# The triangular inverse of each chunk in blocks of 16 joined by products, in a two-layer streaming encoder step

## The chip, the core and the metric

The kernel runs on one core of a Trainium2 chip, as one launch in float32. The metric is device time in microseconds (us); lower is better. TensorE (in the profile PE, its weight loads PEld) multiplies matrices into PSUM; VectorE (DVE), ScalarE (ACT) and GpSimd (POOL) do the elementwise work; SyncE (SP) issues the DMAs. Each engine takes its instructions strictly in the order of the program, and waits on semaphores for those of the others.

## The reference

One step of a streaming encoder with two layers over 1024 prompt tokens and 64 sample tokens, width 1024. Layer 0 is an RWKV-7 time mixing with 16 heads of 64 features and a SwiGLU FFN; layer 1 is windowed attention and another FFN. What matters here is the recurrence of layer 0 (S is a 64 x 64 state for each head):

```python
def step(s, inp):
    r_t, w_t, k_t, v_t, a_t, b_t = inp
    sa = jnp.einsum('bhvk,bhk->bhv', s, a_t)
    s = s * w_t[:, :, None, :] + sa[..., None] * b_t[:, :, None, :] + v_t[..., None] * k_t[:, :, None, :]
    return s, jnp.einsum('bhvk,bhk->bhv', s, r_t)
...
    s_fin, y = lax.scan(step, s0.astype(f32), seq_in)
```

## The kernel before

The 1088 tokens are cut into 17 chunks of 64: eight of the first half of the prompt (A), eight of its second half and one of the sample stream (B). In a chunk the recurrence is solved at once: with T the strict triangle of the products of the b and a vectors, U = W U0, where W = D (I - T D)^-1 and D holds 1 / |kk|^2. So each chunk needs 16 inverses of 64 x 64 triangles, one a head. The heads are held as eight pairs, the even one on partitions 0 to 63 and the odd one on 64 to 127.

For each chunk, `prep` loads the operands, forms the decays and the four triangles of each head (tile `G`, in the code X) by products into PSUM and a mask; `prep2` calls `inverse`, which makes W, and turns the keys (`BT`); `chain` takes the state M through the chunk in four sets of products (U0, Y, U = W U0, the new state); `post` normalises the output Y and turns it back. `recur` runs these so that `prep` and `prep2` of a chunk are emitted beside `chain` and `post` of the chunk ahead.

`inverse` first copies the two diagonal 32 x 32 blocks of each triangle, each four times (`st`, ScalarE, L191), and turns them in blocks of 32 x 32 on VectorE (L196), so that a lane (partition) holds one block and one fourth of its rows: 2 blocks x 16 heads x 4 is 128 lanes. Then it substitutes backwards, two columns at a time, with a multiplication (L216) and a sum (L220) for each of two halves of the rows: 28 of each a chunk. The result is turned back (`WD` and its transpose `XD`) and copied to the diagonal blocks of W. The block beside them comes from two sets of sixteen 32 x 32 products on TensorE: one with the off-diagonal block of T (`N12`, tile `in12`) into `QT`, one with WD into W.

The rest of the kernel is dense work: projections of the time mixing for A, then, beside the recurrence of A, those for B; then, beside the recurrence of B, the output projection and the FFN of A; then attention and the FFNs. Each dense product is three float32r products (lines L422 to L424, PSUM tile `dp`), with the weights split into two parts by ScalarE (L382) and by VectorE or GpSimd (L383).

The order of the instructions on each engine is not written out. A scheduler places them when the program is built, by a priority number and its own estimate of when operands are ready. `recur` gives its products the priority of the stage (1 for A, 3 for B) and most of its other work a lower one (2.5 and 4.5). So a change in one function moves the dense work around it too. A matmul in float32 (not float32r) is recorded twice in the trace.

Lines that the prediction names: L191 (copies into `st`), L196, L198, L205, L206, L208 (turn, scaling, first step and start values), L216 and L220 (substitution), L237 (turn to XD), L247 and L248 (copies of QT), L254 and L255 (last copies into W), L73 and L77 (the helpers through which all products and transposes of the recurrence pass, told apart by tiles: `p_rc` from `r_ixd` are the joins), L110 (norms), L311 (end of the GpSimd part of `post`).

Of the kernel before, what the change touches and what calls it, by code (L numbers as in the profile page):

```python
# [9 lines left out]
F32 = mybir.dt.float32  # L10
# [38 lines left out]
class Rwkv:  # L49
    """The chunked WKV-7 recurrence: chunks of 64 tokens, 16 heads in 8 pairs."""  # L50
# [31 lines left out]
    def start(self):  # L82
        """the part of W that stays zero"""
        nc = self.nc
        self.W = self.sb.tile([128, 8, 64], F32, name="W", tag="W", bufs=1)
        nc.gpsimd.memset(self.W, 0.0)

    def prep(self, ch):
        """all that does not need the state; heads 2j on partitions 0-63, heads 2j + 1 on 64-127"""
# [13 lines left out]
        # 1 / |kk|^2 as the lanes of inverse() hold it: [(parity, half of the tokens, 4 times, pair), token]  # L103
# [30 lines left out]
        # kk a / P and -kk Pex without the norm of kk, whose square inverse() divides by  # L134
# [3 lines left out]
        # r k r_k  # L138
# [3 lines left out]
        # the four triangles of each head: [(b, k) of the key, (a, r) of the query]  # L142
# [10 lines left out]
        # sum(r k r_k) v  # L153
# [7 lines left out]
    def prep2(self, d):  # L161
# [4 lines left out]
        # the strict triangle of b is spent: a takes its place  # L166
# [13 lines left out]
    def inverse(self, X, nl):  # L180
        """D (I - T D)^-1 of the strict triangles T, transposed, with D = 1 / |kk|^2: first the blocks of 32 by
        substitution, a lane for each block and each fourth of its rows, then the block beside them"""
# [4 lines left out]
        st = self.t([128, 1024], "f4", 2)  # L187
        for q in range(4):
            d = 32 * (q % 2)
            src = Xh[d:d + 32, :, q // 2, d:d + 32].rearrange("p j t -> p t j").unsqueeze(2).broadcast_to([32, 32, 4, 8])  # L190
            S.copy(st[32 * q:32 * q + 32].rearrange("p (t g j) -> p t g j", g=4, j=8), src)  # L191
# [370 lines left out]
def tile_stream_step(ctx: ExitStack, tc: tile.TileContext, I, O):  # L562
# [8 lines left out]
    c = {}  # L571
# [841 lines left out]
```

## Time and profile before

| | us |
|---|---|
| three runs | 3085.4, 3092.2, 3096.0 |
| median | 3092.2 |
| span of the profiled execution | 3098.9 |
| TensorE busy | 2948.1 |
| VectorE busy | 1905.6 |
| ScalarE busy | 1371.1 |
| GpSimd busy | 921.6 |

The profiled execution is one run by itself; of its time the profile has only the span, from the first to the last instruction. The profile's groups give for each line and shape the union of the busy time, the mean duration of one and the idle time of the engine ahead of them. Matmuls overlap, so the mean of one is longer than the step from one to the next. The granted clock is the share of TensorE's full clock that its throttle let through.

### The profile page before, as it was taken

Reading aid. Unit: us, or ns where it says so; the run is one execution under the profiler, and the core shown is the slowest. Engines: PE = TensorE matmul, PEld = TensorE weight load, DVE = VectorE, ACT = ScalarE, POOL = GpSimd, SP = SyncE. Lnnn points to the kernel's source line nnn. Section 1 sums busy time; section 2 is a strip of 40 time slices with the busy share of each in tenths; the row PEclk is TensorE's granted clock in tenths of the full one; section 3 lists DMA queues with packets and bytes.
Section 4 is the critical chain, followed back from the end, with each engine's and each line's share of the span. In section 5 each row is a group of like instructions: output and inputs, shape, how many; then the busy total and the mean of one; then the engine's idle time right before and its main releaser. Section 6 shows DMA issues by size and latency. Waiting matters only on the chain. (4 is left out here: it accounts for less than half of the span.)

```text
span 3098.9 us, 52449 instructions
## 1 busy us (share of the span) xinstructions
PE 2948.1 (95%) x20126; PEld 2520.6 (81%) x20126; DVE 1905.6 (61%) x3964; ACT 1371.1 (44%) x2489; POOL 921.6 (30%) x768
## 2 busy tenths in 40 slices
PE   6899898998899999999999999999999999999998
PEld 5677677886677777887778999888667889899998
DVE  8887788968898984356654333565555334633334
ACT  6767655434555442344553222344454233322222
POOL 6464233423333322224311222243111222322221
PEclk9998778988899999999999999999999999999999
DMA  4645443334223224332212222222122332322222
GB/s 143 171 121 152 116 123 91 106 99 143 79 83 96 86 66 127 103 112 84 70 45 69 82 82 82 76 84 82 55 65 65 96 96 75 102 83 83 85 85 69
DMA packets 262051, 289.16 MB, mean 93 GB/s; under 512 B 125028, under 2 KB 143972, under 8 KB 261800
## 3 DMA queue, kind: packets, MB, share of 16 engines
q1 hardware_dynamic: 261800, 285.81, 30.8%
q8 instruction: 158, 2.59, 0.3%
q14 instruction: 93, 0.76, 0.1%
HBM read 243.18 MB, written 41.16 MB: 92 GB/s over the span
## 5 line engine op out<-in xcount | busy, mean ns | idle before, releaser
L422 PE MATMUL dp<-xh,wh 128*128 128x288 f32 (+2 forms) x3480 | 1184.5, 342 | 26.5 <-DVE hx L951 7.0
L423 PE MATMUL dp<-xl,wh 128*128 128x288 f32 (+2 forms) x3480 | 1174.9, 338 | 9.5 <-DVE xl L415 6.9
L424 PE MATMUL dp<-xh,wl 128*128 128x288 f32 (+2 forms) x3480 | 1172.3, 337 | 0.0
L382 ACT CAST wh<-wr 128x512 fp32r<-128x512 f32 x730 | 445.8, 619 | 821.7 <-PE dp L423 635.2
L422 PEld LDWEIGHTS dp<-xh,wh 128*128 128x128 f32 x3480 | 669.2, 193 | 100.5 <-DVE hx L951 9.9
L423 PEld LDWEIGHTS dp<-xl,wh 128*128 128x128 f32 x3480 | 669.9, 193 | 72.3 <-DVE xl L415 8.8
L424 PEld LDWEIGHTS dp<-xh,wl 128*128 128x128 f32 x3480 | 670.2, 193 | 61.4 <-issue 5.6
L383 DVE TENSOR_TENSOR wl<-wr,wh 128x512 fp32r<-128x512 f32 x487 | 377.6, 779 | 444.2 <-ACT wh L382 435.5
L383 POOL TENSOR_TENSOR wl<-wr,wh 128x512 fp32r<-128x512 f32 x243 | 336.0, 1383 | 997.3 <-ACT wh L382 894.1
L422 PE MATMUL dp<-mh,wh 128*128 128x288 f32 (+1 forms) x808 | 255.0, 316 | 3.6 <-DVE hx L951 2.6
L424 PE MATMUL dp<-mh,wl 128*128 128x288 f32 (+1 forms) x808 | 254.6, 315 | 0.0
L423 PE MATMUL dp<-ml,wh 128*128 128x288 f32 (+1 forms) x808 | 253.8, 314 | 0.0
L951 DVE TENSOR_TENSOR a_xB<-dp,a_xB 128x288 f32<-128x288 f32 x352 | 158.1, 456 | 82.4 <-PE dp L424 81.9
L932 DVE TENSOR_TENSOR st<-st,dp 128x288 f32<-128x288 f32 (+1 forms) x132 | 70.0, 531 | 216.8 <-PE dp L424 216.4
L934 POOL TENSOR_TENSOR xl<-st,xh 128x288 fp32r<-128x288 f32 (+1 forms) x102 | 101.2, 993 | 334.2 <-ACT xh L933 322.1
L422 PEld LDWEIGHTS dp<-mh,wh 128*128 128x128 f32 x808 | 152.5, 189 | 13.5 <-DVE hx L951 3.8
L424 PEld LDWEIGHTS dp<-mh,wl 128*128 128x128 f32 x808 | 152.4, 189 | 8.1 <-issue 1.8
L423 PEld LDWEIGHTS dp<-ml,wh 128*128 128x128 f32 x808 | 152.6, 189 | 6.8 <-issue 0.8
L951 DVE TENSOR_TENSOR hx<-dp,hx 128x512 f32<-128x512 f32 x176 | 119.8, 685 | 48.2 <-PE dp L424 47.9
L191 ACT COPY r_f<-r_G 32x1024 f32<-32x1024 f32 x68 | 134.7, 1981 | 32.5 <-DVE r_G L152 21.2
L216 DVE TENSOR_TENSOR r_f<-r_f,r_f 128x60 f32<-128x60 f32 (+5 forms) x476 | 117.5, 278 | 0.5
L930 ACT ACTIVATE st<-dp 128x288 f32<-128x288 f32 (+1 forms) x132 | 62.2, 471 | 93.2 <-PE dp L424 92.8
(344 smaller groups left out, 4003.3 us busy)
## 6 DMA issues: line engine op xcount, KB each, us to landing
wr<-in_ffn_in SPq DMA_DIRECT2D x352, 256.0 KB
wr<-in_ffn_out SPq DMA_DIRECT2D x176, 256.0 KB
wr<-in_rkv SPq DMA_DIRECT2D x90, 256.0 KB
wr<-in_rwo SPq DMA_DIRECT2D x32, 256.0 KB
wr<-in_wq SPq DMA_DIRECT2D x32, 256.0 KB
wr<-in_wo SPq DMA_DIRECT2D x32, 256.0 KB
r_r_s<-s_s SPq DMA_DIRECT2D x17, 256.0 KB
r_sv<-s_vt SPq DMA_DIRECT2D x17, 256.0 KB
```

Of the source, the lines that this page charges most:

```text
L191: S.copy(st[32 * q:32 * q + 32].rearrange("p (t g j) -> p t g j", g=4, j=8), src)
L216: V.tensor_tensor(out=Z[:, h, 1:3, r0:4, 0:j], in0=Z[:, h, a, r0:4, j:j + 2].rearrange("p r c -> p c r").unsqueeze(3).broadcast_to([128, 2 ...
L382: nc.scalar.copy(h, x)
L383: (nc.gpsimd if self.turn % 3 == 0 else nc.vector).tensor_tensor(out=l, in0=x, in1=h, op=ALU.subtract)
L422: self.nc.tensor.matmul(ps, lhsT=wh, rhs=xh, start=i == 0, stop=False)
L423: self.nc.tensor.matmul(ps, lhsT=wh, rhs=xl, start=False, stop=False)
L424: self.nc.tensor.matmul(ps, lhsT=wl, rhs=xh, start=False, stop=i == last)
L930: S.activation(t[o], p, AF.Silu)
L932: V.tensor_tensor(out=t[o], in0=t[o], in1=p, op=ALU.mult)
L934: G.tensor_tensor(out=a.lo[:, q], in0=t[o], in1=a.hi[:, q], op=ALU.subtract)
L951: V.tensor_tensor(out=self.x[m][:, q], in0=p, in1=self.x[m][:, q], op=ALU.add)
```

## The change

The diagonal blocks that are substituted are now 16 x 16: 4 blocks x 16 heads x 2 lanes a block. The copies into `st` and the turn have 512 elements in place of 1024; the lanes of the two blocks of a 32 x 32 square are told apart by masks (`self.e`, made once in `start`). The substitution has seven steps, each one multiplication and one sum over all rows, no longer in two halves. The 16-blocks are joined to 32 by two new sets of 32 products with 16 columns (tile `r_ixd` with X or `in12` into `Q1`, then `Q1` with WD), with a copy by ScalarE between and a sum and a turn by VectorE behind. The joint of 32 to 64 is as before, but takes its operand from X where the heads are even. The constant `xl0` is built on the chip. Comments and docstrings are left out as well. The core of the diff (`...` marks what is left out):

```diff
     def start(self):
         nc = self.nc
-        self.W = self.sb.tile([128, 8, 64], F32, name="W", tag="W", bufs=1)
-        nc.gpsimd.memset(self.W, 0.0)
+        one = lambda shape, n: self.sb.tile(shape, F32, name=n, tag=n, bufs=1)
+        self.W = one([128, 8, 64], "W")
+        self.Q1 = one([128, 8, 32], "Q1")
+        G.memset(self.Q1, 0.0)
+        self.e = one([128, 8], "lanes")
...
-        nl = self.t([128, 32], "nl", 3)
-        V.transpose(out=nl, in_=n4)
+        n2, nl = self.t([128, 32], "n2"), self.t([128, 16], "nl", 3)
+        V.transpose(out=n2, in_=n4)
+        V.tensor_scalar(out=nl, in0=n2[:, 0:16], scalar1=self.e[:, 0:1], scalar2=None, op0=ALU.mult)
+        V.scalar_tensor_tensor(out=nl, in0=n2[:, 16:32], scalar=self.e[:, 1:2], in1=nl, op0=ALU.mult, op1=ALU.add)
...
     def inverse(self, X, nl):
-        st = self.t([128, 1024], "f4", 2)
+        st = self.t([128, 512], "f4", 2)
...
-        N12 = self.t([128, 8, 32], "in12")
-        S.copy(N12[0:32], Xh[0:32, :, 0, 32:64])
-        S.copy(N12[64:96], Xh[0:32, :, 1, 32:64])
+        N1 = self.t([128, 8, 64], "in12")
+        S.copy(N1[64:128], X[0:64, 8:16, 0:64])
...
-        for j in range(30, 0, -2):
+        for j in range(14, 0, -2):
             a, b = (0, 3) if j % 4 else (3, 0)
-            part = [(h, (j // 4 + 1 - h) // 2) for h in range(2) if (j // 4 + 1 - h) // 2 < 4]
-            for h, r0 in part:
-                n = 4 - r0
-                V.tensor_tensor(out=Z[:, h, 1:3, r0:4, 0:j],
...
-            for h, r0 in part:
-                V.tensor_reduce(out=Z[:, h, b, r0:4, 0:j], in_=Z[:, h, min(a, 1):min(a, 1) + 3, r0:4, 0:j].rearrange("p c r j -> p r j c"),
-                                axis=AX.X, op=ALU.add)
+            r0, n = j // 2, 8 - j // 2
+            V.tensor_tensor(out=Z[:, 1:3, r0:8, 0:j],
+                            in0=Z[:, a, r0:8, j:j + 2].rearrange("p r c -> p c r").unsqueeze(3).broadcast_to([128, 2, n, j]),
+                            in1=N0[:, j:j + 2, 0:j].unsqueeze(2).broadcast_to([128, 2, n, j]), op=ALU.mult)
+            V.tensor_reduce(out=Z[:, b, r0:8, 0:j], in_=Z[:, min(a, 1):min(a, 1) + 3, r0:8, 0:j].rearrange("p c r j -> p r j c"),
+                            axis=AX.X, op=ALU.add)
...
+        for e in range(2):
+            V.tensor_scalar(out=XX.rearrange("p (r s) -> p r s", r=8)[:, :, 16 * e:16 * e + 16], in0=XL, scalar1=self.e[:, e:e + 1], scalar2=None, op0=ALU.mult)
...
+        turn()
...
+        ps = self.pc()[:, 0:128].rearrange("p (a b) -> p a b", a=8)
+        for j in range(8):
+            for q in range(4):
+                o = slice(32 * q, 32 * q + 32)
+                self.mm(ps[o, j, :], lhsT=T(q, j, slice(o.start % 64, o.start % 64 + 32)), rhs=XD[o, j, 0:16], start=True, stop=True)
+        S.copy(Q1[:, :, 0:16], ps)
+        ps = self.pc()[:, 0:128].rearrange("p (a b) -> p a b", a=8)
+        for j in range(8):
+            for q in range(4):
+                o = slice(32 * q, 32 * q + 32)
+                self.mm(ps[o, j, :], lhsT=Q1[o, j, :], rhs=WD[o, j, 16:32], start=True, stop=True)
+        V.tensor_tensor(out=WD[:, :, 16:32], in0=ps, in1=WD[:, :, 16:32], op=ALU.add)
+        turn()
+        V.tensor_scalar(out=W[:, :, 0:32], in0=WD, scalar1=self.e[:, 2:3], scalar2=None, op0=ALU.mult)
+        S.activation(W[:, :, 32:64], WD, AF.Copy, scale=self.e[:, 3:4])
...
-    for n in ("tri", "mask", "bd", "xl0"):
+    for n in ("tri", "mask", "bd"):
```

What this does to the order is seen at three places. First VectorE, in the substitution of a chunk of the second half, before (`r_f` are the tiles NL and Z of the code; the last number is the shape of what is written):

```order
L216 TENSOR_TENSOR r_f_518_9089<-r_f_518_9089,r_f_517_9086 128x2x3x8
L216 TENSOR_TENSOR r_f_518_9089<-r_f_518_9089,r_f_517_9086 128x2x3x4
L220 TENSOR_REDUCE r_f_518_9089<-r_f_518_9089 128x3x8
L220 TENSOR_REDUCE r_f_518_9089<-r_f_518_9089 128x3x4
L216 TENSOR_TENSOR r_f_518_9089<-r_f_518_9089,r_f_517_9086 128x8x6
L216 TENSOR_TENSOR r_f_518_9089<-r_f_518_9089,r_f_517_9086 128x8x2
L220 TENSOR_REDUCE r_f_518_9089<-r_f_518_9089 128x4x6
L220 TENSOR_REDUCE r_f_518_9089<-r_f_518_9089 128x4x2
```

and in such a chunk of the changed kernel (L420 splits a weight of the FFN, L318 copies U):

```order
L237 TENSOR_REDUCE r_f_612_9831<-r_f_612_9831 128x2x12
L234 TENSOR_TENSOR r_f_612_9831<-r_f_612_9831,r_f_611_9827 128x2x3x10
L237 TENSOR_REDUCE r_f_612_9831<-r_f_612_9831 128x3x10
L234 TENSOR_TENSOR r_f_612_9831<-r_f_612_9831,r_f_611_9827 128x2x4x8
L237 TENSOR_REDUCE r_f_612_9831<-r_f_612_9831 128x4x8
L234 TENSOR_TENSOR r_f_612_9831<-r_f_612_9831,r_f_611_9827 128x2x5x6
L420 TENSOR_TENSOR wl_12257<-wr_12258,wh_12256 128x512
L237 TENSOR_REDUCE r_f_612_9831<-r_f_612_9831 128x5x6
L234 TENSOR_TENSOR r_f_612_9831<-r_f_612_9831,r_f_611_9827 128x2x6x4
L237 TENSOR_REDUCE r_f_612_9831<-r_f_612_9831 128x6x4
L318 COPY r_sv_9691<-p_rc_9731 64x8x64
```

Two steps of each kind before each result was used have become one. Over the whole program VectorE has 3326 instructions in place of 3964.

Then TensorE at the joins, before, in the second half (`p_rc` from `r_ixd` is a join; `p_ry` belongs to `chain`):

```order
L422 MATMUL dp_11805<-xh_11200,wh_11799 128x512
L73 MATMUL p_ry_8953<-r_M_8689,r_AR_8555 64x64 x16
L73 MATMUL p_rc_8830<-r_ixd_8801 32x32
L423 MATMUL dp_11805<-xl_11201,wh_11799 128x512
L424 MATMUL dp_11805<-xh_11200,wl_11800 128x512
L422 MATMUL dp_11805<-xh_11206,wh_11799 128x512
L73 MATMUL p_rc_8954<-r_sv_8949,r_G_8567 64x64 x16
L73 MATMUL p_rc_8830<-r_ixd_8801 32x32 x15
```

and in the changed kernel, from the end of the first new set of products past the second (`Q` is Q1, `p_rp` from `r_AR` makes the triangles of the next chunk):

```order
L73 MATMUL p_rc_9478<-r_ixd_9474,r_in_565_9444 32x16 x2
L73 MATMUL p_rp_9623<-c_bd,r_rt_9620 64x2 x8
L73 MATMUL p_rp_9662<-r_AR_9649,r_BK_9650 128x128 x4
L459 MATMUL dp_12097<-xh_11691,wh_12091 128x512
L460 MATMUL dp_12097<-xl_11692,wh_12091 128x512
L461 MATMUL dp_12097<-xh_11691,wl_12092 128x512
L73 MATMUL p_rc_9512<-r_ixd_9474,Q_2522 32x16 x32
L73 MATMUL p_rp_9663<-r_AR_9649,r_BK_9650 128x128 x4
L73 MATMUL p_rp_9674<-r_AR_9649,r_BK_9650 128x128 x4
```

Between the two new sets stand eight small products, four of the triangles and three dense ones; TensorE has 18350 instructions in place of 17262.

Third, the dense products between chunks, counted in TensorE's order from the last product of U of one chunk to that of another:

| | before | changed |
|---|---|---|
| first to eighth chunk (A) | 986 | 603 |
| eighth to ninth | 236 | 629 |
| ninth to seventeenth (B) | 913 | 572 |

The dense work is the same; less of it stands beside the recurrence and more behind it.

More of the change, by code (lines that the diff above doesn't have):

```diff
@@ new lines, in inverse @@
+        one = N0[:, 32:512:66]
+        N0 = N0.rearrange("p (t s) -> p t s", t=16)
+        NL = N0[:, :, 0:16]
+        V.scalar_tensor_tensor(out=NL, in0=NL, scalar=self.e[:, 0:1], in1=N0[:, :, 16:32], op0=ALU.mult, op1=ALU.add)
+        V.tensor_tensor(out=NL, in0=NL, in1=mid(nl, 16), op=ALU.mult)
+        ev = N0.rearrange("p (a two) b -> p a two b", two=2)[:, :, :, 0:16]
+        Z = self.t([128, 4, 8, 16], "f4", 2)
+        tm = Z[:, 0]
+        V.tensor_tensor(out=tm, in0=bc(one, 16), in1=ev[:, :, 0, :], op=ALU.mult)
@@ new lines, in inverse @@
+            V.tensor_reduce(out=Z[:, b, r0:8, 0:j], in_=Z[:, min(a, 1):min(a, 1) + 3, r0:8, 0:j].rearrange("p c r j -> p r j c"),
+                            axis=AX.X, op=ALU.add)
+        XL = Z[:, 0]
+        q4 = lambda x: x.rearrange("p r (q f) -> p r q f", f=4)[:, :, :, 0:2]
+        V.tensor_copy(q4(XL), q4(Z[:, 3]))
+        xe = XL.rearrange("p r (a two) -> p r a two", two=2)
+        tm = Z[:, 1, :, 0:8]
+        V.tensor_tensor(out=tm, in0=xe[:, :, :, 1], in1=mid(one, 8), op=ALU.mult)
```

69 lines of the change are left out of this document (31 added, 38 removed).

## The prediction

> **What bounds the kernel now.** I read the page first: its span, the busy shares, and its forty slices.
>
> ```profile
> span 3098.9 us, 52449 instructions
> ...
> PE 2948.1 (95%) x20126; PEld 2520.6 (81%) x20126; DVE 1905.6 (61%) x3964; ACT 1371.1 (44%) x2489; POOL 921.6 (30%) x768
> ...
> DVE  8887788968898984356654333565555334633334
> ...
> PEclk9998778988899999999999999999999999999999
> ```
>
> TensorE is busy 95% of the span. VectorE is nearly full only in the first 16 slices, and only there does the granted clock fall: that is where the recurrence runs. The profiled execution has a span of 3098.9 us, 6.7 above the median of the three times (3092.2); no other time of it is given. I sum the change in us and add it to the median.
>
> VectorE's timeline shows when the last piece of each chunk's inverse W is written (L255; start, length), 17 times:
>
> ```profile
> 343.84 0.42 DVE L255 COPY W<-p_rc 32x256 f32<-32x256 f32 x1 [0.24 <-ACT W L254]
> ...
> 1173.52 0.42 DVE L255 COPY W<-p_rc 32x256 f32<-32x256 f32 x1 [0.29 <-ACT W L254]
> ```
>
> The eighth ends at 672, the ninth, which opens the second half, at 788. So I cut the span at these four times and asked for the busy time of each stretch (columns: stretch, length, then busy us of PE, PEld, DVE, ACT, POOL, then granted clock).
>
> ```profile
> 265.00:344.00 79.00, 63.80 (x517) 54.87 (x516) 55.71 (x145) 55.98 (x84) 21.68 (x21) 0.81 0.48 145
> 344.00:672.00 328.00, 308.36 (x3115) 266.50 (x3115) 271.26 (x750) 179.41 (x289) 109.05 (x77) 0.84 0.39 106
> 672.00:788.00 116.00, 93.48 (x640) 73.64 (x638) 85.41 (x173) 51.65 (x73) 38.24 (x29) 0.82 0.44 126
> 788.00:1174.00 386.00, 373.46 (x3276) 287.64 (x3276) 347.76 (x922) 192.86 (x266) 133.26 (x100) 0.93 0.27 84
> ...
> 1217.00:1317.00 100.00, 100.00 (x433) 81.20 (x431) 37.44 (x54) 28.66 (x48) 23.73 (x19) 1.00 0.44 128
> 2700.00:2800.00 100.00, 100.00 (x753) 100.00 (x752) 38.36 (x76) 26.16 (x50) 20.72 (x19) 1.00 0.26 83
> ```
>
> Two stretches are start-ups (265 to 344 and 672 to 788), in which one chunk is prepared with none to run beside it. Two are steady: seven chunk periods of the first half (A), eight of the second (B). The last two rows are dense work alone: 0.231 us for a matmul of 512 columns, 0.133 for one of 288. With these rates I take the dense work out of a steady stretch. Two groups of TensorE of the first steady stretch, then one of the second:
>
> ```profile
> L422 PE MATMUL dp<-xh,wh 128*128 128x290 f32 x284 | 95.0, 337 | 4.6 <-ACT st L792 4.6
> ...
> L752 PE MATMUL dp<-xh,wl 64*128 64x290 f32 x16 | 8.2, 515 | 0.0
> ...
> L422 PE MATMUL dp<-xh,wh 128*128 128x512 f32 x294 | 126.5, 432 | 6.5 <-DVE st L932 4.0 <-DVE hx L951 2.5
> ```
>
> A holds three groups like the first (852) and six like the second (96): 948 at 0.133 are 126 us, so 328 - 126 = 202 us, 28.9 a chunk, go to the recurrence. B holds three like the third (880): 203 us, which leaves 183, or 22.9 a chunk. The recurrent work of a chunk is the same in both. TensorE stands idle 328 - 308.4 = 19.6 us in A (2.8 a chunk) and 12.5 in B (1.6); the rest of the difference goes with the clock, 0.84 against 0.93. So TensorE bounds both, and VectorE, at 83% and 90%, sets some of A's waits.
>
> **The change, part by part.** What goes is VectorE's and ScalarE's (groups of the whole span):
>
> ```profile
> L216 DVE TENSOR_TENSOR r_f<-r_f,r_f 128x60 f32<-128x60 f32 (+5 forms) x476 | 117.5, 278 | 0.5
> ...
> L220 DVE TENSOR_REDUCE r_f<-r_f 128x30 f32<-128x90 f32 (+5 forms) x476 | 97.9, 237 | 0.8
> ...
> L208 DVE TENSOR_TENSOR r_f<-c_xl,r_nl 128x256 f32<-128x256 f32 x34 | 26.1, 808 | 0.3
> ...
> L198 DVE TENSOR_TENSOR r_f<-r_f,r_nl 128x1024 f32<-128x1024 f32 x17 | 25.0, 1470 | 0.2
> ...
> L196 DVE STREAM_TRANSPOSE r_f<-r_f 128x1024 f32<-128x1024 f32 x17 | 21.1, 1243 | 34.8 <-ACT r_f L191 34.8
> ...
> L237 DVE STREAM_TRANSPOSE r_ixd<-r_ixd 128x256 f32<-128x256 f32 x17 | 7.5, 440 | 0.4
> ...
> L191 ACT COPY r_f<-r_G 32x1024 f32<-32x1024 f32 x68 | 134.7, 1981 | 32.5 <-DVE r_G L152 21.2
> ```
>
> The substitution goes from 28 multiplications and 28 sums a chunk to 7 and 7: three quarters of 215 us, or 161. The rows of 1024 and 256 elements shrink to half or a quarter: of their 72 us some 35 go. The new masks, a third turn (440 ns by L237) and the add from PSUM give about 25 back. VectorE is thus relieved of about 170 us, 10 a chunk. The substitution is now one dependent sequence, no longer two halves in turn; in the order other work of VectorE stands between some of its steps, and where none does a step waits for the one ahead, in room that VectorE then has. ScalarE's four copies halve: 67 us, 4 a chunk. None of this is time by itself where TensorE is full. SyncE loses one constant's load; the once-only preparation of the lanes (a dozen small VectorE instructions) stands beside dense work at 265 us; I cost both at nothing. Without that cover the preparation would be some 3 us.
>
> What comes is TensorE's: 96 small products a chunk in place of 32, so 1088 more. The nearest row is the present block of sixteen 32x32 products (x32 because each is recorded twice):
>
> ```profile
> 1141.78 1.22 PE L73 MATMUL p_ry<-r_M,r_AR 64*64 64x64 f32 x22
> 1142.93 0.69 PE L73 MATMUL p_rc<-r_ixd,r_in 32*32 32x32 f32 x32
> 1143.56 0.33 PE L77 MATMUL p_rp<-c_id,r_BK 64*128 64x64 f32 x2
> ...
> 586.85 1.06 PE L73 MATMUL p_rc<-r_ixd,r_in 32*32 32x32 f32 x32
> ```
>
> From its start to the next start it takes 0.63 us at the full clock and 0.99 at half. For 64 more that is 2.5 us a chunk, or 4.0 at half clock. The new ones have half the columns and lie on four row groups in place of two: at best half the price, 1.25. They can't cost less than nothing, since each is issued in order. I take 2.0, nearer the row: **+34 us** for 17 chunks (21 to 56, most chunks being at the full clock).
>
> By the Trainium skill, TensorEngine Tiling (Array Packing), Tiling Modes, Key Properties, a change of the tiling mode drains the engine. In the rows above the block begins 0.07 us before the one ahead of it ends, and so does the one behind it, so the trace shows no such drain at these two edges. By the rule two more blocks would bring four more drains a chunk; at 0.19 us each, the length of one product, that would be 13 us more.
>
> The new joins also add two waits to each inverse: TensorE for ScalarE's copy of Q1, and for VectorE's sum and turn. In the order of the changed program, products of the next chunk's G and a few dense ones stand between, so I cost them at nothing; without that cover each is about one copy of 0.4 us, 14 us in all.
>
> What goes of TensorE's waits, from its waits in three stretches (us in all, times, longest):
>
> ```profile
> PE p_ry L77 <- POOL r_yc L311: 5.5, 1, 5.5
> PE p_rc L73 <- ACT r_ixd L247: 4.7, 1, 4.7
> PE p_rc L73 <- DVE r_ixd L237: 3.0, 1, 3.0
> ...
> PE p_rc L73 <- DVE r_ixd L248: 2.0, 1, 2.0
> ...
> PE p_rc L73 <- DVE r_ixd L237: 2.6, 1, 2.6
> ...
> PE dp L422 <- ACT st L792: 4.6, 1, 4.6
> PE dp L423 <- DVE xl L415: 4.1, 1, 4.1
> PE p_rp L73 <- DVE r_n L110: 3.3, 1, 3.3
> ```
>
> The first four are of the second start-up, the fifth of the first, the last three of A. Waits that name the inverse are 4.7 + 3.0 + 2.0 + 2.6 = 12.3; they should mostly go. Those of A are for work that stands in the two queues behind the substitution, 12.0; I take two thirds. Late next in A is the chain through POOL to the transposes (5.5 above). Together **-20 us** (nothing to -45: both start-ups' idle 37.7 and part of A's).
>
> What moves: the changed order lets chunks follow with less dense work between, 603 dense matmuls in place of 986 in A's seven periods and 572 in place of 913 in B's eight. The 383 and 341 moved run later, without a recurrence beside them: 51 us at a clock of 0.84 and 79 us at 0.93 go to nearly 1.0. If the slow windows hit all work alike, that saves 51/0.84 - 51 + 79/0.93 - 79 = 16 us. If they belong to the chunks, what remains is hit harder and nothing is saved. I take half, **-8** (-16 to +24, see the second rival).
>
> Sum: 34 - 20 - 8 = +6, so 3092 + 6 = **3098 us**.
>
> **The rivals.** *VectorE paces the first half.* For it: A's 28.9 against B's 22.9, and VectorE at 83% with most of A's waits in queues it shares. Then A falls to B's price with the new products, 24.9: 7 x -4 = -28; B loses its idle 1.6 but pays 2.0: +3; start-ups -20 + 4; moved work -8. That is -49: 3043 us. Against it: waits on VectorE make up only part of A's 19.6 us idle.
>
> *The clock falls (the slower side).* With less dense work a chunk, TensorE's time is more of small products and of waits. For it: A has less dense work a chunk than B (126/7 = 18 us against 25) and the lower clock. B's dense share comes down to 572 x 0.231 / 8 = 16.5 us, below A's now. If its clock goes with that to A's 0.84, its chunks go to A's 28.9: 8 x 6 = +48, with 34 - 20 that is 3154; half way, at 0.885, it is 3130. I price it at 3140. It decides from a clock below about 0.90 in B's stretch. Against it: A has more idle time, which the change should cut.
>
> By the Trainium skill, TensorE: Matmul & The Clock Gate, Why this matters for your kernels, gaps of more than about 3 us between bursts bring the clock back to half. The rows agree in kind: the clock is lowest in the stretches with most idle time.
>
> *VectorE isn't relieved at all* can't be: the order has 638 fewer instructions there.
>
> **How the numbers follow.** Forecast 0.45, first rival 0.33, second 0.22. A measurement of this kernel can tell about 0.3%, 9 us, from no change. The forecast's own range, 3080 to 3125, crosses zero: of its 0.45 I put 0.07 on faster, 0.20 on the same, 0.18 on slower. So faster 0.40, same 0.20, slower 0.40. The range reaches to both rivals, 3035 to 3145; out of it are the first with cheap products and the second at its full price.
>
> **What would show it.** The windows between ends of W: A's price a chunk near 28, B's near 25, and PE's small products 2 us a chunk more. A's price near 25 bears out the first rival; a clock under 0.90 in B's stretch the second. The 16-column blocks much under 0.3 us or over 0.7 would make the first term wrong; waits of TensorE on Q1, on the turned tile or on the transposes, over 1 us a chunk, would make my cover wrong.

## The result, and the profile after

The changed kernel takes 3132.7 us (median of three, 3130.6 to 3137.8) where the kernel before took 3092.2: a ratio of 1.0137, with a 95% interval of 1.0114 to 1.0159. It is slower by 40 us, which is clear of the noise. Its page, in the lines that answer to those shown of before (the span, the busy times, VectorE's forty slices and the granted clock in tenths):

```profile
span 3130.9 us, 56228 instructions
...
PE 2988.9 (95%) x22302; PEld 2559.7 (82%) x22302; DVE 1783.6 (57%) x3326; ACT 1309.7 (42%) x2476; POOL 905.3 (29%) x769
...
DVE  8787768638777753356654333565464434633334
...
PEclk9998867999777899999999999999999999999999
```

VectorE lost 122 us of busy time and ScalarE 61, so the relief came. TensorE gained 41 us. The clock's row has sevens where eights and nines stood before, and a six where a seven stood. The steady stretches, cut as in the prediction at the ends of W (stretch, length, busy us of PE, PEld, DVE, ACT, POOL, granted clock):

```profile
341.30:634.00 292.70, 268.73 (x3622) 226.49 (x3622) 206.09 (x451) 143.38 (x251) 87.15 (x68) 0.80 0.36 98
...
787.80:1137.70 349.90, 332.95 (x4031) 257.84 (x4032) 260.64 (x564) 142.51 (x222) 114.71 (x89) 0.83 0.24 74
```

With the dense work taken out at the prediction's rates (603 x 0.133 and 572 x 0.231 us), a chunk of the first half costs 30.4 us (28.9 before) and one of the second 27.2 (22.9 before). The clock in the second half's chunks fell from 0.93 to 0.83. The prediction had put 28 and 25 as the marks of its forecast. TensorE's idle time in the two stretches went up, from 19.6 and 12.5 us to 24.0 and 17.0; what it waits for there (us in all, times, longest), first in the first half, then in the second:

```profile
PE p_rc L73 <- DVE r_sv L318: 7.6, 4, 3.3
PE p_rc L73 <- DVE W L292: 5.0, 3, 3.7
PE p_rc L73 <- DVE r_iqt L285: 4.6, 1, 4.6
...
PE p_rp L73 <- DVE r_n L126: 4.4, 2, 3.5
PE p_ry L77 <- POOL r_yc L348: 3.0, 3, 1.6
PE p_rc L73 <- ACT Q L268: 3.0, 1, 3.0
```

These are single gaps at many places, in the inverse and in the chain alike; no one wait took the place of the old ones.

**A balance for every kernel.** Two numbers of each profiled run turned out to carry nearly all differences: the time in which TensorE does nothing (span less busy time, both on the page), and the time lost to the clock (span times one less the mean granted clock over the span). The rows for the clock:

```profile
core 0: 3098.9 us, clock 0.952
```

```profile
core 0: 3130.9 us, clock 0.946
```

The first is the kernel before: 3098.9 - 2948.1 = 150.8 us idle, 3098.9 x 0.048 = 148.7 lost to the clock. The second is the changed kernel: 142.0 idle, 169.1 lost. The third part is the added products' own time: from the first start of each block of them to the start of what follows it, idle time in the block and behind it taken off, summed over the trace. One such block in the changed kernel, at half clock (start, length; each product is recorded twice):

```profile
947.36 0.63 PE L461 MATMUL dp<-xh,wl 128*128 128x512 f32 x1
947.91 1.05 PE L73 MATMUL p_rc<-r_ixd,Q 32*32 32x16 f32 x64
948.89 4.08 PE L73 MATMUL p_rp<-r_AR,r_BK 64*128 64x128 f32 x16
```

It counts 948.89 - 947.91 = 0.98 us. All 34 blocks of the changed kernel come to 27.0 us. From before to after the balance says -8.8 (idle) + 20.4 (clock) + 27.0 (products) = 38.6; the spans differ by 32.0. The clock's part is an upper estimate, since not all work runs at half speed at half clock (the block above takes 0.98 us there and about 0.7 at the full clock), and part of it is in the products' own time already.

How much of it is time is seen in runs of one and the same program, whose order doesn't change from run to run: the runs of the kernel before that were made beside the experiments lie between 3082.7 us at a granted clock of 0.963 and 3103.1 us at 0.952. Over all 117 runs that have a clock on record, each compared with the others of its kernel on its chip, the time goes up by about 20 us where the clock is 0.01 lower; the balance charges 31. So the clock goes with the time when the order is held fixed, and about two thirds of the balance's clock column is time.

### The profile page after: what moved, and what is told of

Its sections match the earlier page's. It is cut to its first block, busy times and chain, and to the rows that moved or that the text cites. A ratio compares the mean times of both kernels' runs of the same rounds, so it can differ in the third digit from the quotient of the medians.

```text
span 3130.9 us, 56228 instructions
## 1 busy us (share of the span) xinstructions
PE 2988.9 (95%) x22302; PEld 2559.7 (82%) x22302; DVE 1783.6 (57%) x3326; ACT 1309.7 (42%) x2476; POOL 905.3 (29%) x769
## 5 line engine op out<-in xcount | busy, mean ns | idle before, releaser
L420 DVE TENSOR_TENSOR wl<-wr,wh 128x512 fp32r<-128x512 f32 x487 | 375.5, 774 | 502.5 <-ACT wh L419 493.2
L420 POOL TENSOR_TENSOR wl<-wr,wh 128x512 fp32r<-128x512 f32 x243 | 334.3, 1376 | 1060.2 <-ACT wh L419 938.7
L459 PEld LDWEIGHTS dp<-mh,wh 128*128 128x128 f32 x808 | 153.0, 189 | 10.1 <-issue 2.4
L73 PE MATMUL p_rp<-r_AR,r_BK 64*128 64x128 f32 x544 | 100.8, 362 | 14.1 <-DVE r_n L126 6.7
L73 PEld LDWEIGHTS p_rp<-r_AR,r_BK 64*128 64x128 f32 x544 | 85.9, 256 | 23.7 <-issue 13.3
L970 ACT CAST xh<-st 128x288 fp32r<-128x288 f32 (+1 forms) x102 | 50.2, 492 | 121.9 <-DVE st L969 120.8
```

The lines of the kernel that those rows point to most:

```text
L73: self.nc.tensor.matmul(*a, **k)
L420: (nc.gpsimd if self.turn % 3 == 0 else nc.vector).tensor_tensor(out=l, in0=x, in1=h, op=ALU.subtract)
L459: self.nc.tensor.matmul(ps, lhsT=wh, rhs=xh, start=i == 0, stop=False)
L970: S.copy(a.hi[:, q], t[o])
```

## The experiments

The expectations name or number their theories each for itself. The table gathers all runs; ratios are to the kernel before on the same chips, with 95% intervals; "idle", "clock" and "own" are the three parts of the balance, in us, and the last two columns compare their sum with the span, both as differences from *cut*, the fastest. The span is that of the one profiled execution, which lies up to 12 us off its kernel's median.

| kernel | median us | ratio | span | idle | clock | own | sum over cut | span over cut |
|---|---|---|---|---|---|---|---|---|
| before | 3092.2 | 1 | 3098.9 | 150.8 | 148.7 | 0 | 45 | 46 |
| changed | 3132.7 | 1.0137 [1.0114, 1.0159] | 3130.9 | 142.0 | 169.1 | 27 | 84 | 78 |
| half_steps | 3075.9 | 0.9945 [0.9927, 0.9963] | 3085.2 | 134.5 | 148.1 | 0 | 28 | 33 |
| twice | 3173.8 | 1.0256 [1.0228, 1.0284] | 3172.0 | 141.9 | 196.7 | 61 | 145 | 120 |
| paced_b | 3163.2 | 1.0219 [1.0194, 1.0244] | 3158.2 | 134.9 | 157.9 | 26 | 64 | 106 |
| wide_b | 3137.4 | 1.0131 [1.0098, 1.0165] | 3123.8 | 132.1 | 137.4 | 24 | 39 | 71 |
| cut | 3047.6 | 0.9845 [0.9821, 0.9868] | 3052.5 | 126.4 | 128.2 | 0 | 0 | 0 |
| four_wide | 3074.1 | 0.9928 [0.9902, 0.9954] | 3076.8 | 120.1 | 132.3 | 14 | 11 | 24 |
| loose | 3130.4 | 1.0119 [1.0080, 1.0159] | 3135.0 | 145.0 | 178.7 | 24 | 93 | 83 |
| warm | 3129.7 | 1.0105 [1.0082, 1.0129] | 3119.4 | 121.2 | 137.3 | 69 | 73 | 67 |
| loose_one | 3090.3 | 1.0000 [0.9985, 1.0015] | 3087.9 | 138.6 | 148.2 | 12 | 44 | 35 |
| beside | 3095.7 | 1.0015 [1.0000, 1.0031] | 3090.6 | 134.6 | 132.9 | 30 | 43 | 38 |
| packed | 3126.5 | 1.0128 [1.0103, 1.0154] | 3119.5 | 119.5 | 146.6 | 59 | 70 | 67 |
| ranked | 3124.1 | 1.0108 [1.0083, 1.0132] | 3122.9 | 139.0 | 153.0 | 33 | 70 | 70 |

**half_steps.** The kernel before with the first half of its substitution's steps left out (its inverse is another), so VectorE is relieved and no product is added:

```
-        for j in range(30, 0, -2):
+        for j in range(14, 0, -2):
```

> The kernel before with 7 of its 15 substitution steps (half of the substitution is left out): VectorE is relieved by some 120 us, no product is added, and the order packs the chunks closer by itself (831 dense matmuls between the chunks of the first half in place of 986, 710 in place of 913 in the second). Theory 1, the clock falls because chunks follow each other with less dense work between: no gain in spite of the relief, 3085 to 3105, with a granted clock of about 0.88 in the second half's chunks (0.93 before). Theory 2, the added products are the cost: without them the relief shows, 3065 to 3080, clock unchanged.

It took 3075.9 us, 18 less than the kernel before beside it, and the second half's clock stayed at 0.92: theory 2. A chunk of the first half came down to (294.9 - 831 x 0.133) / 7 = 26.3 us, one of the second to (341.9 - 710 x 0.231) / 8 = 22.2. Relief of VectorE is worth time, mostly in the first half, though the order left a chunk less dense work than before (831 and 710 dense matmuls in place of 986 and 913).

**twice.** The changed kernel with each of the 64 new products issued twice, into the same place (shown for the second set, the first likewise):

```
-                self.mm(ps[o, j, :], lhsT=Q1[o, j, :], rhs=WD[o, j, 16:32], start=True, stop=True)
+                for _ in range(2):
+                    self.mm(ps[o, j, :], lhsT=Q1[o, j, :], rhs=WD[o, j, 16:32], start=True, stop=True)
```

> The changed kernel with each of the 64 new products of a chunk issued twice, into the same place: 1088 more small products, nearly the same order (570 and 595 dense matmuls between chunks). Theory 2, the products are the whole of the loss: as much again, +35 to +45 on the changed kernel, about 3172. Theory 1: only their own issue, 0.02 us each by the blocks of 32 in 0.66 us, so +22, about 3155, clock in the chunks unchanged.

3173.8 us, as theory 2 had it: 41 more than the changed kernel for 1088 more products, 38 ns each. Their own time rose by 61 - 27 = 34, so once the products stand there, most of what more of them cost is their issue time. The balance adds 28 us for the clock here and overshoots the span by 25; at 20 us for each 0.01 the clock would add 16.

**paced_b and wide_b.** The changed kernel with TensorE's priorities in the second half spread over the dense work's, so that more of it comes between the chunks (935 and 1427 dense matmuls in place of 572):

```
-                rw.two.at(base + 0.301 + late, low + 0.301 + late)
+                rw.two.at(pe(i, 0.301), low + 0.301 + late)
...
-    M = recur(range(8, 16), M, 3, LOW[1])
+    M = recur(range(8, 16), M, 3, LOW[1], (4.0, 0.0003))
```

(0.0002 in paced_b; the other two places of the kind go the same way.)

> The changed kernel with the priority of the recurrent products of the second half set so that 935 dense matmuls stand between its chunks (913 in the kernel before, 572 in the changed one); nothing else changes. Theory 1: the clock in these chunks comes back to about 0.93 and the loss of the second half goes: 3132 - 30 = about 3102. Theories 2 and 3 (the new waits at the joins are the cost): 3125 to 3135, no change, since products and waits are all there.

> As the paced one, but with 1427 dense matmuls between the chunks of the second half, so nearly all of the FFN stands among them. Theory 1: each window of time has more dense work, the clock is above 0.93 there, and the time is below the paced one's, 3085 to 3100. Theories 2 and 3: 3125 to 3135. If the chunks now end after the dense work that hides them, slower than 3135.

Neither is faster than the changed kernel: 3163.2 and 3137.4 us. The clock did come back in the second half of wide_b:

```profile
777.00:1322.10 545.10, 535.83 (x4854) 401.73 (x4851) 341.95 (x674) 204.85 (x318) 159.19 (x123) 0.94 0.25 81
```

Taken alone this looked like the end of the clock as an explanation. The balance shows what hid it: both spans lie 42 and 32 us over the sum of the three parts. What these two have most of is changes between dense and recurrent work on TensorE: in the second half's chunks 381 and 312, against 102 in the changed kernel, 106 in cut and 134 before. That is 275 and 206 more than in cut, and 42/275 and 32/206 are both about 0.15 us a change. The steps in the changed kernel's trace are of that order: at the full clock a dense matmul of 512 columns that is followed by a recurrent product takes 326 ns to the next start, where one followed by another dense one takes 232.

**cut, four_wide, loose, warm.** These take the change apart. *cut* removes the join of 16 to 32 whole:

```
-                self.mm(ps[o, j, :], lhsT=T(q, j, slice(o.start % 64, o.start % 64 + 32)), rhs=XD[o, j, 0:16], start=True, stop=True)
-        S.copy(Q1[:, :, 0:16], ps)
...
-                self.mm(ps[o, j, :], lhsT=Q1[o, j, :], rhs=WD[o, j, 16:32], start=True, stop=True)
-        V.tensor_tensor(out=WD[:, :, 16:32], in0=ps, in1=WD[:, :, 16:32], op=ALU.add)
-        turn()
```

> Leaves out both new sets of 32 small products with what hangs on them (the copy of Q1, the sum, the third turn): the blocks of 16 aren't joined to 32. VectorE's relief stays, and the order is as thin as the changed kernel's (633 and 635 dense matmuls in the steady stretches, against 603 and 572; the kernel before has 986 and 913). Theory 1, the added products cost what doubling them cost (41 us): 3132.7 - 41 = 3092, and lower only as far as waits went with them. Theory 2, the join's waits cost some 17 us more on top of the products: 3075, as with half of the substitution. Theory 3, the thin order lets the clock fall whether products are added or not: clock in the second half's chunks stays below 0.88 and the time over 3085, with the work of a chunk beside the dense part near 25 us there.

```profile
span 3052.5 us, 51794 instructions
...
PE 2926.1 (96%) x20126; PEld 2510.7 (82%) x20126; DVE 1767.9 (58%) x3292; ACT 1304.3 (43%) x2457; POOL 905.8 (30%) x769
...
core 0: 3052.5 us, clock 0.958
...
337.00:598.20 261.20, 247.30 (x2772) 210.31 (x2771) 200.51 (x445) 143.37 (x250) 86.10 (x66) 0.84 0.39 112
745.30:1061.50 316.20, 308.55 (x2997) 238.66 (x2997) 256.81 (x562) 143.66 (x218) 110.51 (x88) 0.90 0.26 83
```

3047.6 us, lower than any theory had it, and 85 under the changed kernel. A chunk costs (261.2 - 633 x 0.133) / 7 = 25.3 us in the first half and (316.2 - 635 x 0.231) / 8 = 21.2 in the second, with nearly as little dense work a chunk as in the changed kernel. So the thin order alone doesn't make the kernel slower, though the second half's clock fell with it from 0.93 to 0.90. Without the join the relief is worth 47 us against the kernel before beside it (3095.0); by the balance it is 24 of idle time and 20 of clock.

*four_wide* keeps the join's steps but takes four products of 128 columns for each set of 32 (each uses the first pair's block for all pairs):

```
-        for j in range(8):
-            for q in range(4):
+        for q in range(4):
...
-                self.mm(ps[o, j, :], lhsT=Q1[o, j, :], rhs=WD[o, j, 16:32], start=True, stop=True)
+            self.mm(ps[o], lhsT=Q1[o, 0, :], rhs=WD[o, :, 16:32], start=True, stop=True)
```

> Each new set of 32 products of 16 columns becomes four of 128 columns over the same rows, results and operands (each takes the first pair's block for all pairs, so W is another): the waits, the copy, the sum, the third turn and the changes of the array's tiling stay, the number of products goes from 96 a chunk to 40. The order gives the steady stretches 907 and 777 dense matmuls, nearly as before the change. Number of products is what costs: near 3080 (cut plus a few us). Waits and tiling changes at the joins are what costs: 3105 to 3125. Thin dense work is what costs: the clock in the second half's chunks is back over 0.90 and the time with it, 3070 to 3085; this run can't tell that from the number, cut can.

3074.1 us: with copy, sum, third turn and both waits in place it is 27 over cut, 14 of them own time. Its order has more dense work a chunk than cut's (907 and 777 matmuls), so the two don't compare in the order alone; but with every wait of the join in place there is no 50 us to be found.

*loose* is the counterpart: all 64 products, none of the waits.

```
-        S.copy(Q1[:, :, 0:16], ps)
...
-                self.mm(ps[o, j, :], lhsT=Q1[o, j, :], rhs=WD[o, j, 16:32], start=True, stop=True)
+                self.mm(ps[o, j, :], lhsT=T(q, j, slice(o.start % 64, o.start % 64 + 32)), rhs=WD[o, j, 16:32], start=True, stop=True)
-        V.tensor_tensor(out=WD[:, :, 16:32], in0=ps, in1=WD[:, :, 16:32], op=ALU.add)
-        turn()
```

> Issues both sets of 32 products right after the first turn, into PSUM that nobody reads; the copy of Q1, the sum and the third turn go, so TensorE waits for nothing between the sets. W is without the join. The order's dense work is as thin as the changed kernel's (555 and 593). Number of products: 3120 to 3135, as the changed kernel. Waits at the joins: as cut, within 10 us. Both in part: in the middle.

3130.4 us, the changed kernel's time. Without any wait of the join, the products and the order that the scheduler drew up around them bring back all 83 us. The clock of its two steady stretches is 0.76 and 0.84:

```profile
335.00:625.90 290.90, 269.19 (x3585) 227.66 (x3584) 196.19 (x439) 140.10 (x245) 83.60 (x65) 0.76 0.34 97
785.60:1149.50 363.90, 340.41 (x4068) 267.38 (x4067) 265.16 (x561) 143.29 (x218) 121.65 (x94) 0.84 0.23 76
```

Over cut it has 24 us of own time, 19 of idle time and up to 50 of clock (30 at 20 us for each 0.01).

*warm* asks whether the clock is a cause. The changed kernel gets eight more products a chunk that fill the whole array:

```
+    def keep(self, bank, x, n):
+        for _ in range(n):
+            self.mm(bank.rearrange("p a b -> p (a b)")[:, 0:128], lhsT=self.c["bd"], rhs=x, start=True, stop=True)
...
+            self.keep(ps[0], BK[:, 0], 2)
...
+        self.keep(ps, X[:, 0, :], 2)
...
+        self.keep(Sp, U0[:, 0:2, :], 2)
```

> The changed kernel with eight extra 128x128 products of 128 columns a chunk, two at each of four places in its stretches without dense work (ahead of the state's update, of the first join and of each half of the four triangles), into PSUM that is overwritten right after; results stay. By themselves they add 8 x 0.23 us and some six changes of tiling at 0.1 us: 2.4 us a chunk, 41 us, of which waits of up to 1 us a chunk hide 17: 3132.7 + 24 = 3157 if the clock doesn't matter. If the low clock after stretches of small products is what costs, the clock rises above 0.90 in both halves and gives back some 40 us or more: at or under 3125.

```profile
span 3119.4 us, 56769 instructions
...
PE 2998.2 (96%) x22574; PEld 2576.5 (83%) x22574; DVE 1772.7 (57%) x3326; ACT 1309.4 (42%) x2474; POOL 906.9 (29%) x769
...
core 0: 3119.4 us, clock 0.956
...
336.50:620.30 283.80, 272.04 (x3702) 231.09 (x3701) 204.73 (x450) 144.50 (x250) 86.64 (x67) 0.82 0.35 100
786.20:1133.40 347.20, 336.94 (x4158) 264.93 (x4157) 252.16 (x559) 143.60 (x222) 114.27 (x89) 0.88 0.23 75
```

The 136 products took 44 us of TensorE's time by their starts, and the kernel is no slower: 3129.7 us. Idle time fell by 21 us (part of them ran in waits), and what the clock loses by 32. That is between the two expectations, nearer to the clock's. The clock of the steady stretches rose from 0.80 and 0.83 to 0.82 and 0.88, under the 0.90 that was expected. With the runs of one program above it is the evidence that the low clock costs real time: work that is good for nothing is paid back by a higher clock and by idle time that it fills. The order is another here too, so the shares of the two aren't exact.

**loose_one, beside, packed.** *loose_one* is loose with the first set alone.

> As loose, but with the first of its two sets of 32 products alone (544 more than cut in place of 1088); the join is left out here too. If the price goes with the number, half of the 83 us between cut and loose: 3089. If the price is each set's own issue time, 0.66 us for 32, with a lower clock only from a certain length of a stretch without dense work on: near 3065. If it is the order with little dense work between the products (582 and 579 dense matmuls, as thin as loose's 555 and 593): near 3125.

3090.3 us, half of the price, as by number. *beside* is cut with all 64 products at the end of the inverse, on the finished W:

```
         V.tensor_copy(W[64:96, :, 32:64], ps[64:96])
+        for _ in range(2):
...
+                    self.mm(ps[o, j, :], lhsT=W[o, j, 32:64], rhs=W[o, j, 0:16], start=True, stop=True)
```

> cut with 64 products of 32x32 with 16 columns a chunk, as many as loose has, but on the finished W at the end of the inverse, beside the products of the next chunk that need W; nobody reads them, and the join is left out. Price by number wherever they stand: 3130, as loose. Price by what they make of the order and of the stretches without dense work: another time, 3075 to 3110, with the clock in the second half's chunks over loose's 0.84 and the idle time of TensorE under loose's 45 us in the two steady stretches.

```profile
336.00:623.10 287.10, 265.30 (x3622) 224.57 (x3621) 200.39 (x449) 142.25 (x250) 84.85 (x65) 0.81 0.36 101
778.30:1112.40 334.10, 323.30 (x4093) 255.08 (x4094) 261.00 (x573) 149.11 (x222) 115.47 (x92) 0.91 0.26 82
```

3095.7 us: as many products of the same shape, more own time (30 us against 24), and 35 us less than loose. The clock of the second half is 0.91. So the price doesn't depend on the number alone, but on where the products stand and on the order that results.

*packed* computes the same join with 24 larger products:

```
+                o = slice(64 * par, 64 * par + 64)
+                self.mm(ps[o, j, :], lhsT=N1[o, j, :] if par else X[o, j, 0:64], rhs=XB[o, j, :], start=True, stop=True)
...
+            self.mm(ps[:, j, :], lhsT=Q1[:, j, :], rhs=WD[:, j, 16:32], start=True, stop=True)
```

> The same join with 24 products in place of 64: the first set as sixteen of 64x64 with 32 columns (the operand spread over two column groups by two masked copies), the second as eight of 128x128 with 16 columns (Q1's blocks copied onto a diagonal). Results stay. If the number of products is what costs, 24/64 of 83 us, 31, on cut's 3048 with the join's waits and five more small copies a chunk at 0 to 15: 3079 to 3094, at or under the time before the change, and near four_wide's 3074. If the joins' waits cost, as little gain over the changed kernel as they are the same or longer: 3115 to 3135.

3126.5 us; fewer products did not help. That is the time that was expected if the waits cost, but the trace shows another reason. The group of its second set between 345 and 1140 us:

```profile
L73 PE MATMUL p_rc<-r_ixd,Q 128*128 128x16 f32 x240 | 36.3, 293 | 0.9 <-DVE Q L273 0.9
```

Their starts lie 144 ns apart on average for a record of 128x128 with 16 columns (112 at the full clock), where those of 32x32 with 16 columns lie 12 apart. Both sets come to 59 us of own time, twice the changed kernel's. The small products are the cheap form; this attempt at a faster version failed.

**ranked.** The changed kernel with one priority changed, so that TensorE's products of the inverse rank behind those of the next chunk's triangles:

```
-                rw.two.at(base + 0.1 + late, base + 0.1 + late)
+                rw.two.at(base + 0.35 + late, base + 0.1 + late)
```

> The changed kernel with one number changed: TensorE's products of the inverse rank behind those of the next chunk's triangles (priority 0.35 in place of 0.1). Every product, wait and result stays; in the order the dense work stands in more, shorter pieces between the products (17 or 18 stretches of small products in a chunk would be cut by 8 to 11 blocks of dense work where 7 cut them now; 603 and 757 dense matmuls in the steady stretches). If the products cost what they cost wherever they stand: 3125 to 3135. If beyond their own 27 us it is the clock after long stretches without dense work: mean clock over the whole span from 0.946 to 0.951 or more and 3095 to 3115, less some 3 to 6 us for 28 more changes of tiling.

```profile
343.10:649.20 306.10, 278.43 (x3621) 231.86 (x3622) 205.58 (x450) 139.35 (x247) 85.66 (x68) 0.77 0.33 94
804.20:1174.70 370.50, 359.90 (x4212) 277.14 (x4213) 276.77 (x581) 156.60 (x243) 122.26 (x97) 0.91 0.25 80
```

3124.1 us, 9 below the changed kernel in the median, with overlapping intervals; the span is 8 shorter. The clock's theory came true by half. The mean clock reached its 0.951, but the time lies just under the range of the other theory: with the same products the second half's clock rose from 0.83 to 0.91, but that of the first half fell from 0.80 to 0.77. Over the span the clock loses 16 us less, and the products' own time rose by 6, as their blocks are cut into more pieces. No version with the whole computation beat the kernel before.

**What makes the clock fall.** The clock's records change on a grid of 3.41 us. Six windows of this grid in the changed kernel's second half, first all work, then the dense matmuls alone (columns as above):

```profile
946.59:950.00 3.41, 3.41 (x72) 2.63 (x73) 3.18 (x11) 3.15 (x6) 0.00 (x0) 0.50 0.32 90
950.00:953.41 3.41, 3.41 (x14) 2.95 (x14) 3.34 (x12) 0.51 (x1) 1.57 (x1) 0.50 0.00 0
953.41:956.82 3.41, 3.41 (x25) 2.19 (x23) 0.66 (x2) 2.15 (x2) 1.12 (x2) 0.50 0.00 0
956.82:960.23 3.41, 3.41 (x39) 2.40 (x38) 0.20 (x1) 0.00 (x0) 0.00 (x0) 1.00 0.00 0
960.23:963.64 3.41, 3.41 (x20) 2.63 (x13) 2.62 (x5) 0.36 (x1) 0.00 (x0) 0.50 0.19 68
963.64:967.06 3.42, 3.42 (x8) 2.32 (x8) 2.66 (x4) 1.77 (x3) 1.11 (x1) 0.50 0.56 170
```

```profile
946.59:950.00 3.41, 1.39 (x3) 0.58 (x3) 0.00 (x0) 0.00 (x0) 0.50 0.32 90
950.00:953.41 3.41, 0.50 (x1) 0.50 (x2) 0.00 (x0) 0.00 (x0) 0.50 0.00 0
953.41:956.82 3.41, 2.43 (x6) 1.32 (x4) 0.00 (x0) 0.00 (x0) 0.50 0.00 0
956.82:960.23 3.41, 0.00 (x0) 0.00 (x0) 0.00 (x0) 0.00 (x0) 1.00 0.00 0
960.23:963.64 3.41, 0.27 (x1) 0.34 (x1) 0.00 (x0) 0.00 (x0) 0.50 0.19 68
963.64:967.06 3.42, 3.42 (x7) 2.32 (x8) 0.69 (x1) 0.00 (x0) 0.50 0.56 170
```

TensorE is busy in all of them; there is no idle time. The window from 953.41 has 2.43 us of dense work, and the next one runs at the full clock. That next one has none, only transposes and small products, and the one after it is at half. For a count, take the windows between the first and the last end of W in the kernels before and changed, and give each matmul the time from its start to the next start, or to its own end. Of 49 windows at the full clock with under a fifth of dense work 34 were followed by one at half clock, of 48 with a fifth to two fifths 11, and of 242 with more 1. The kernel before has 32 windows with under a fifth of dense work in that time, the changed kernel 67, loose 67, cut 35.

Gaps without work play a part in that: of the 49 windows only 24 were busy throughout, and 14 of these were followed by half clock. What separates the windows better than dense work or idle time is how much of the array the products use. Weight each product's time by the share of the 128x128 array that its shape takes (a 32*32 product takes a sixteenth; products that run side by side are not added up), and take only windows at the full clock in which TensorE was never idle, from all fourteen kernels:

| mean share of the array in use | windows | followed by half clock |
|---|---|---|
| under 0.3 | 65 | 61 |
| 0.3 to 0.4 | 72 | 50 |
| 0.4 to 0.5 | 105 | 33 |
| over 0.5 | 1753 | 26 |

Between its ends of W the changed kernel has 51 windows (busy or not, at either clock) with a share under 0.4, loose 59 and twice 68; the kernel before has 32 and cut 30. warm has 39 and beside 43. That links the small products to the clock.

By the Trainium skill, TensorE: Matmul & The Clock Gate, Why this matters for your kernels, it is gaps without work that bring the clock back to half. These rows show another case: a window full of small products counts like a gap. No run was made to vary the share alone, so the limit is known only as far as this table goes.

## Why the prediction was off, step by step

The forecast was 3098, within 3080 to 3125; the whole range, 3035 to 3145, holds 3132.7, and slower had a chance of 0.40. The forecast's own range doesn't hold it; the wider one does because it reaches to the second rival, so that the time lies inside is in part luck. Where the sum had +34 for products, -20 for waits and -8 for moved work, the balance from before to after has +27, -9 and +20 at most.

- **The products, +34.** As issue time this was right, or a little high: 27 us, and 34 for as many again in *twice*. As a price it was far too small. cut and loose show +83 in the place where the change puts them, with the order that comes with it. The step that failed is that the term counted the products' own time only. What they bring besides, up to 50 us of clock and 19 of idle time, had no term of its own.
- **TensorE's waits, -20.** Without the join it was right: idle time falls by 24 us in cut. With the products 16 of it come back, so the term came out at -9. The waits that name the inverse were to mostly go; from the first start-up to the last end of W they went up from 16 us to 25.
- **The new waits of the join, nothing.** Nearly right: loose, which has none, takes the same time. The waits for Q1's copy come to the one of 3.0 us shown above, and those for the turned tiles to 6.8 us, where the kernel before has 6.5.
- **The moved dense work, -8, within -16 to +24.** This term held all that was said of the clock, and the clock's part came out at +20. The bound on the bad side was right and its reason was not: the prediction looked for the clock's fall in dense work that becomes thin. cut has nearly as thin an order and loses 20 us less to the clock than the kernel before.
- **The tiling's changes.** The two edges quoted in the prediction lie between recurrent products and showed no drain. Between dense and recurrent work there is a longer step, 0.09 us by the starts and 0.15 by the balance. It doesn't explain this result, as the changed kernel has fewer such edges (102 against 134 in the second half's chunks), but it would account for what wide_b lost. By the Trainium skill, TensorEngine Tiling (Array Packing), Key Properties, a change of mode drains the engine; at the edges between dense and recurrent work the trace agrees in kind, at the two of the prediction it doesn't.
- **The first rival, VectorE paces the first half,** was right in part. It gave a chunk of the first half 24.9 us with the products; cut shows 25.3 without them, 3.6 less than before, where the second half's chunk lost 1.7. The gain was there and was spent.
- **The second rival, the clock falls,** came nearest: it was decided by a clock under 0.90 in the second half, which was 0.83. That its 3130 at half way lies by the measured time is luck: for a clock of 0.84 it had 3154, with 28.9 us for a chunk, which was 27.2. That TensorE's time is then more of small products is what the windows show; that less dense work a chunk brings the fall by itself is not, as cut shows.
- **VectorE's relief** was 122 us in place of 170. Of the 48 missing, 20 are in the substitution, which takes 74 us where three quarters off left 54. In the mean a step of 48 elements takes longer than before, first before and then after:

```profile
L216 DVE TENSOR_TENSOR r_f<-r_f,r_f 128x48 f32<-128x48 f32 x102 | 25.2, 247 | 0.1
```

```profile
L234 DVE TENSOR_TENSOR r_f<-r_f,r_f 128x48 f32<-128x48 f32 x34 | 14.6, 430 | 0.7
```

But 25 of the 34 take 197 to 212 ns, as the median of 200 before. The other nine take 776 to 1302 ns, and each of them ran while GpSimd had an operation, as here:

```profile
381.30 1.04 POOL L158 TENSOR_TENSOR r_rkr<-r_rkr,vecs 128x512 f32<-128x512 f32 x1
381.63 0.78 DVE L234 TENSOR_TENSOR r_f<-r_f,r_f 128x48 f32<-128x48 f32 x1
```

In the kernel before it is the same: all 39 multiplications of L216 over 400 ns ran beside GpSimd's work. The sums, with one operand, never took over 304 ns. So it isn't that the shorter sequence's steps are slower: fewer steps are left, and a larger part of them met GpSimd (28 of 119 against 39 of 476).

What stays open: each edit also gives the scheduler another order, and no two runs here have the same one. ranked and beside show that place and order, with as many products, move the clock's loss by 16 and 46 us; how much of loose's loss is due to the products standing in a row, and how much to the order drawn up around them, could not be told apart. The price of the clock rests on runs of the same program, its cause on the count of windows; no run changed the one with all else fixed. That wide_b's regained clock went into changes of tiling follows from the balance, not from a run made for it.

## What to carry to other kernels

Work that moves from a slack engine to small products on TensorE should be priced twice: by the issue time, and by how many windows of 3.4 us it makes in which the products use little of the array (here under some 0.4). Before such a change, take the granted clock in windows of that length and see what stands in the windows ahead of the slow ones. And test a gain by leaving the new part out altogether (cut): it shows at once what the relief is worth and what the replacement costs.

## What the runs showed of the hardware that was not expected

- Windows of 3.41 us in which TensorE was busy throughout, but whose products used under 0.3 of the array, were followed by half clock in 61 of 65 cases; with over 0.5 in 26 of 1753.
- Runs of one and the same program differ by about 20 us for each 0.01 of granted clock (3082.7 us at 0.963, 3103.1 at 0.952).
- VectorE's multiplication of 48 elements a lane took some 0.2 us in 25 cases and 0.78 to 1.30 us in the nine in which GpSimd worked.
- 136 extra products of 128x128, 44 us of TensorE's time, left the kernel's time where it was, with a clock of 0.956 in place of 0.946 over the span and 21 us less idle time.
- Products of 32x32 with 16 columns start 12 ns apart on average (two records each), those of 128x128 with 16 columns 144 ns apart: with so few columns the full array was the dearer form.
